# A Strassen-type output product: three pairs held for the closing part, in another order of the products

## The chip, the cores and the metric

The kernel runs on one core of a Trainium2 chip. It has a matrix engine (PE in the profile, with its weight loads as PEld), a vector engine (DVE), an activation engine (ACT), GpSimd (POOL) and SyncE (SP), which here issues nearly all transfers. The metric is the device time of one execution in microseconds; less is better.

## The reference

One transformer-like layer on x of 512 tokens by 1024, in float32. The change lies in the last line, in the product with `ffn2_w_out` (2816 by 1024):

```python
def swiglu(u, w_in, w_out):
    a, b = jnp.split(u @ w_in, 2, axis=-1)
    return (jax.nn.silu(a) * b) @ w_out
...
    u = rms_norm(x, ffn2_norm_g) * (1 + sc3) + sh3
    x = x + 0.5 * g3 * swiglu(u, ffn2_w_in, ffn2_w_out)
    return x
```

## The kernel before, in words

Every float32 product is made of three matrix products: each operand is split into a part `hi` (ACT copies it to the short float format) and a rest `lo` (DVE subtracts `hi` from the source), and `mm3` (L106) accumulates hi·hi, hi·lo and lo·hi, as lines L108, L109 and L110.

The second feed-forward block uses fewer products than the plain scheme. The hidden dimension of 2816 has 22 blocks of 128 rows, taken as 11 pairs, `i` = 0 to 10 (`NP` = 11). The tokens are taken as two halves of 256 and the output columns as two halves of 512. `pair_out` (L443) runs in two phases. In the first, three products are accumulated over the 11 pairs; their combinations P1, U2 and U4 stay on the chip. In the second phase four more products Z, Y, X and W are accumulated over the pairs, each into two PSUM banks (`tb` = 0, 1: 128 tokens by 512 columns), Z and Y in the pool `t`, X and W in the pool `g`. This second phase is what the change touches.

For each pair `prepare(i)` (L487) makes two weight tiles of 128 by 2 by 512. Tile `c` is a block of rows of the weight; its two halves feed Z and Y. Tile `d` comes from a scratch in DRAM (`ws`) with sums of weights made earlier; its halves feed W and X. Each of the two takes a load of 512 KB into a `raw` buffer, an ACT copy for `hi` and a DVE subtraction for `lo`, both in `split` (L82; ACT at L89, DVE at L91). There are 3 `raw` buffers, and 4 buffers each for `wh` and `wl`. A `raw` buffer comes free when the DVE subtraction that reads it is done. The other operand of pair `i` is `A2[i]`, which lies in a place of its own, named `A0` to `A10` (hp pool, tag `A{i}`, with a single buffer each); that place is not read any more once the second phase has gone through pair `i`.

One `step(n, tb, i, o)` is one `mm3`: three matmuls. A pair has 4 products by 2 banks, thus 24 matmuls. Pairs 0 to 8 are run one after the other. The last two pairs (`tail = 2`, L504) are the closing part: both are prepared, and then each bank gets its steps of both pairs and is finished. For a finished bank `add(src, half, tbs)` (L497) scales it with the gate (one DVE `SCALAR_TENSOR_TENSOR` at L499 from PSUM) and adds it to the residual x (one DVE `TENSOR_TENSOR` at L501 for each place), and `store` (L502) sends the finished part of x to the output (SP, L503). Z goes to one half of the columns, Y to the other, X is needed in both halves, W in one; the parts of x that X and W add to are the same for the first half.

The order in which the instructions of an engine stand is made by the scheduler of the tile framework, which moves instructions by its own estimate of when they are ready; each engine then runs its list in that order.

Of the kernel before, what the change touches and what calls it, by code (L numbers as in the profile page):

```python
# [12 lines left out]
F32R = mybir.dt.float32r  # L13
# [7 lines left out]
P = 128  # L21
# [25 lines left out]
class Layer:  # L47
# [31 lines left out]
            self.last_raw = self.nc.sync.dma_start(dst(t), src)  # L79
        return t  # L80

    def split(self, src, shape):  # L82
        nc = self.nc
        hi = self.wp.tile(shape, F32R, name=self.nm("wh"), tag="wh", bufs=4)
        lo = self.wp.tile(shape, F32R, name=self.nm("wl"), tag="wl", bufs=4)

        after = lambda i: self.tc.issue_after(i.ins) if self.lo_after else nullcontext()
        with after(self.last_uf):
            nc.scalar.activation(hi, src, AF.Copy)  # L89
        with after(self.last_ul):  # L90
            nc.vector.tensor_tensor(lo, src, hi, op=SUB)  # L91
        return hi, lo
# [350 lines left out]
    def pair_out(self, w, v, hp, tp, x_src):  # L443

        nc = self.nc
        V = nc.vector.tensor_tensor
        NP = NJ // 2
        slots = iter([f"{a}{k}" for k in range(NK) for a in ("uh", "ul")])
        new = lambda n: self.up.tile([P, 512], F32, name=self.nm(n), tag=next(slots))
        def two(*src):  # L450

            n = 2 // len(src)
            t = self.raw([P, 2, 512], [(lambda t, i=i: t[:, i:i + n, :] if n > 1 else t[:, i, :], a) for i, a in enumerate(src)])
            return self.split(t, [P, 2, 512])
        both = lambda r: w[r * P:(r + 1) * P, :].rearrange("p (h n) -> p h n", h=2)
        def one(src):
            t = self.tmp(tp, "raw1")
            nc.sync.dma_start(t, src)
            return self.split(t, [P, 512])
        def mm(ps, tb, a, b, start, stop):  # L460
            s = slice(tb * P, (tb + 1) * P)
            self.mm3(ps[tb], a[0][:, s], a[1][:, s], b[0], b[1], start, stop)

        Z, Y = [[self.tbank() for _ in range(2)] for _ in range(2)]
        X = [self.gbank() for _ in range(2)]
        for i in range(NP):
            wh, wl = two(w[2 * i * P:(2 * i + 1) * P, 0:512], self.ws[i][:, 0, :])
            w2 = one(self.ws[i][:, 2, :])
            A1 = self.A1[i]
            for ps, n, b in ((Z, 0, (wh[:, 0, :], wl[:, 0, :])), (X, 2, w2), (Y, 1, (wh[:, 1, :], wl[:, 1, :]))):  # L470
                for tb in range(2):
                    mm(ps, tb, (A1[:, n, :], A1[:, 3 + n, :]), b, i == 0, i == NP - 1)
            if i:
                self.pair_split(i - 1, hp, tp)
        P1, U2, U4 = [[new(n) for _ in range(2)] for n in ("P1", "U2", "U4")]
        for tb in range(2):
            nc.scalar.activation(P1[tb], Z[tb], AF.Copy)
        for tb in range(2):
            V(U2[tb], X[tb], P1[tb], op=ADD)
        for tb in range(2):  # L480
            V(U4[tb], Y[tb], U2[tb], op=ADD)
        self.pair_split(NP - 1, hp, tp)

        W, X = [[self.gbank() for _ in range(2)] for _ in range(2)]
        Z, Y = [[self.tbank() for _ in range(2)] for _ in range(2)]
        banks = {"Z": Z, "Y": Y, "X": X, "W": W}
        def prepare(i):  # L487
            c, d = two(both(2 * i + 1)), two(self.ws[i][:, 1:4:2, :])
            A2 = self.A2[i]
            a = lambda n: (A2[0][:, n, :], A2[1 + n // 2][:, n % 2, :])  # L490
            b = lambda n: ((c, d)[n // 2][0][:, n % 2, :], (c, d)[n // 2][1][:, n % 2, :])
            return {"Z": (a(0), b(0)), "Y": (a(3), b(1)), "X": (a(2), b(3)), "W": (a(1), b(2))}
        step = lambda n, tb, i, o: mm(banks[n], tb, *o[n], i == 0, i == NP - 1)
        g = [new("gb") for _ in range(2)]
        for h in range(2):
            nc.sync.dma_start(g[h], self.mod_d[v:v + 1, h * 512:(h + 1) * 512].to_broadcast([P, 512]))
        def add(src, half, tbs):  # L497
            t = self.tmp(tp, "rs")
            nc.vector.scalar_tensor_tensor(t, src, 0.5, g[half], op0=MUL, op1=MUL)  # L499
            for tb in tbs:  # L500
                V(self.x[tb][half], self.x[tb][half], t, op=ADD)  # L501
        def store(tb, half):  # L502
            nc.sync.dma_start(self.out[0, tb * P:(tb + 1) * P, half * 512:(half + 1) * 512], self.x[tb][half])  # L503
        tail = 2  # L504
        for i in range(NP - tail):
            o = prepare(i)
            for n in ("WZXY" if i == 0 else "ZYXW"):
                for tb in range(2):
                    step(n, tb, i, o)
            if i == 4:  # L510
                self.x_tiles()
                x_src()
            if i in (6, 7):
                tb = i - 6
                add(P1[tb], 0, (tb,))
                add(U2[tb], 0, (tb + 2,))
                add(U4[tb], 1, (tb, tb + 2))
        os = [prepare(i) for i in range(NP - tail, NP)]
        for n in "ZYXW":
            for tb in range(2):  # L520
                for i, o in enumerate(os):
                    step(n, tb, NP - tail + i, o)
                ps = banks[n][tb]
                if n == "Z":
                    add(ps, 0, (tb,))
                    store(tb, 0)
                elif n == "Y":
                    add(ps, 1, (tb,))
                    store(tb, 1)
                elif n == "X":  # L530
                    add(ps, 1, (tb + 2,))
                    store(tb + 2, 1)
                    add(ps, 0, (tb + 2,))
                else:
                    add(ps, 0, (tb + 2,))
                    store(tb + 2, 0)

    def token_gemm(self, lhs, nk, w, half, done, tail=2, extra=None, last=None):

# [801 lines left out]
```

## Time and profile before

| | |
|---|---|
| Time, median of 3 runs | 1352.87 us (1352.03 to 1353.68) |
| Profiled execution, its own time | 1351.66 us |
| Its span in the trace | 1349.8 us |
| PE busy | 1326.3 us, 98% of the span |
| DVE busy | 888.9 us, 66% |
| ACT busy | 586.0 us, 43% |
| Granted PE clock, mean | 0.998 |

The busy time of an engine counts the instructions that the profile shows on it; a matmul is shown longer than the distance between two, so the distance of the starts is what counts for PE. In the rows of the timeline the first number is the start, the second the duration, and a bracket at the end says how long the engine had been idle before and what ended that.

### The profile page before, as it was taken

How to read it: one execution, taken by the hardware profiler on the slowest of the kernel's cores; microseconds unless marked ns; L12 is line 12 of the kernel's file. 1: busy time of each engine (PE TensorE's matmuls, PEld its weight loads, DVE VectorE, ACT ScalarE, POOL GpSimd, SP SyncE). 2: the span in 40 equal slices, each digit the busy share in tenths (PEclk: the TensorE clock that was granted, in tenths of full speed). 3: DMA queues.
4: the chain of work that ended last, by engine and by line, in shares of the span. 5: the costliest groups of instructions: out<-in, count | busy, mean ns of one | idle time of the engine just before them, and what ended most of it. 6: DMA issues, size and time to landing. Idle time of an engine off the chain costs nothing.

```text
span 1349.8 us, 17806 instructions
## 1 busy us (share of the span) xinstructions
PE 1326.3 (98%) x6500; PEld 1110.5 (82%) x6500; DVE 888.9 (66%) x1668; ACT 586.0 (43%) x977; POOL 43.2 (3%) x67
## 2 busy tenths in 40 slices
PE   7999999999999999999999999999999999999997
PEld 6788887887879888888888888888788888888886
DVE  6866666655558757978786876446475555545776
ACT  4532333322235655556565676333253232223732
POOL 2000000000011011000000000002010000000000
PEclk9999999999999999999999999999999999999999
DMA  9675656665635343444243442364436777764574
GB/s 289 189 225 183 185 179 211 218 203 180 203 90 121 111 125 110 135 132 124 64 140 90 133 128 73 114 195 141 145 108 185 221 231 222 222 196 137 168 240 166
DMA packets 247291, 220.36 MB, mean 163 GB/s; under 512 B 13282, under 2 KB 208514, under 8 KB 247204
## 3 DMA queue, kind: packets, MB, share of 16 engines
q1 hardware_dynamic: 246820, 219.15, 54.1%
q8 instruction: 51, 0.84, 0.3%
q14 instruction: 36, 0.29, 0.1%
q0 software_dynamic: 320, 0.06, 0.0%
q10 hardware_dynamic: 64, 0.02, 0.0%
HBM read 195.00 MB, written 24.19 MB: 162 GB/s over the span
## 4 chain that ended last, share of the span: by engine, by line
PE 86%; DVE 7%; ACT 3%; DMA 3%; issue 1%; SPq 0%; DVEq 0%; ACTq 0%
PE g L110 23%; PE g L108 23%; PE g L109 23%; PE t L108 3%; PE t L109 3%; PE t L110 3%; PE g L693 2%; DVE wl L91 2%; PE t L1066 1%; PE t L1036 1%; DMA x<-x_d 1%; PE t L1007 1%; ACT wh L89 1%; DMA raw<-in_ffn_w_out_dram 1%; PE t L1008 1%
## 5 line engine op out<-in xcount | busy, mean ns | idle before, releaser
L89 ACT ACTIVATE wh<-raw 128x1024 fp32r<-128x1024 f32 (+2 forms) x237 | 244.4, 1036 | 434.9 <-PE g L109 144.3
L91 DVE TENSOR_TENSOR wl<-raw,wh 128x1024 fp32r<-128x1024 f32 (+2 forms) x237 | 290.3, 1227 | 190.0 <-ACT wh L89 171.0
L110 PE MATMUL g<-uh,wl 128*128 128x512 f32 (+1 forms) x976 | 366.5, 376 | 1.3 <-DVE wl L91 1.2
L108 PE MATMUL g<-uh,wh 128*128 128x512 f32 (+1 forms) x976 | 367.3, 377 | 0.2 <-ACT wh L89 0.2
L109 PE MATMUL g<-ul,wh 128*128 128x512 f32 (+1 forms) x976 | 366.5, 376 | 0.1
L110 PEld LDWEIGHTS g<-uh,wl 128*128 128x128 f32 x976 | 183.4, 188 | 35.5 <-DVE wl L91 2.2
L109 PEld LDWEIGHTS g<-ul,wh 128*128 128x128 f32 x976 | 183.6, 188 | 33.2 <-POOL ul L243 0.4
L108 PEld LDWEIGHTS g<-uh,wh 128*128 128x128 f32 x976 | 183.5, 188 | 33.2 <-ACT wh L89 0.8
L108 PE MATMUL g<-wh,uh 128*128 128x512 f32 (+2 forms) x320 | 112.3, 351 | 0.0
L110 PE MATMUL g<-wh,ul 128*128 128x512 f32 (+2 forms) x320 | 111.5, 349 | 0.0
L109 PE MATMUL g<-wl,uh 128*128 128x512 f32 (+2 forms) x320 | 111.4, 348 | 0.0
L280 DVE SCALAR_TENSOR_TENSOR acc<-raw,ccol,acc 128x1024 f32<-128x1024 f32 x49 | 62.8, 1282 | 15.4 <-DMA raw<-in_w_ada_dram 14.9
L108 PEld LDWEIGHTS g<-wh,uh 128*128 128x128 f32 x320 | 60.5, 189 | 7.8 <-DVE tk L913 0.5
L110 PEld LDWEIGHTS g<-wh,ul 128*128 128x128 f32 x320 | 60.4, 189 | 7.7
L109 PEld LDWEIGHTS g<-wl,uh 128*128 128x128 f32 x320 | 60.5, 189 | 7.3
L108 PE MATMUL g<-yh,wh 128*128 128x512 f32 x128 | 50.4, 394 | 0.0
L110 PE MATMUL g<-yh,wl 128*128 128x512 f32 x128 | 50.2, 392 | 0.0
L109 PE MATMUL g<-yl,wh 128*128 128x512 f32 x128 | 49.7, 388 | 0.0
L1018 ACT ACTIVATE S<-S,mn 128x128 f32<-128x128 f32 (+1 forms) x64 | 35.6, 557 | 16.8 <-DVE mn L1010 8.4
L109 PE MATMUL t<-wl,A 128*128 128x512 f32 x88 | 34.3, 390 | 0.8 <-DVE wl L91 0.8
L108 PE MATMUL g<-wh,hh 128*128 128x512 f32 x88 | 35.0, 398 | 0.0
L110 PE MATMUL g<-wh,hl 128*128 128x512 f32 x88 | 34.9, 397 | 0.0
(319 smaller groups left out, 2054.1 us busy)
## 6 DMA issues: line engine op xcount, KB each, us to landing
raw<-in_ffn_w_in_dram SPq DMA_DIRECT2D x82, 512.0 KB
raw<-in_w_ada_dram SPq DMA_DIRECT2D x56, 512.0 KB
raw<-in_w_mix_dram SPq DMA_DIRECT2D x46, 512.0 KB
raw<-in_ffn_w_out_dram SPq DMA_DIRECT2D x33, 512.0 KB
s<-in_ffn_w_out_dram SPq DMA_DIRECT2D x44, 256.0 KB
ws<-s SPq DMA_DIRECT2D x22, 512.0 KB
raw<-in_w_mix_dram SPq DMA_DIRECT2D x33, 256.0 KB
ar<-in_w_ada_dram SPq DMA_DIRECT2D x32, 256.0 KB
```

Source lines behind the costliest of these rows:

```text
L89: nc.scalar.activation(hi, src, AF.Copy)
L91: nc.vector.tensor_tensor(lo, src, hi, op=SUB)
L108: mm(ps, lh, rh, start=start, stop=False)
L109: mm(ps, lh, rl, start=False, stop=False)
L110: self.last_mm = mm(ps, ll, rh, start=False, stop=stop)
L280: nc.vector.scalar_tensor_tensor(acc, r, self.ccol[:, k:k + 1], acc, op0=MUL, op1=ADD)
L693: mm = nc.tensor.matmul(acc_ps[b], (wl if p == 1 else wh)[:, b % 2, s], self.ul[k] if p == 2 else self.uh[k], start=k == 0 and p == 0, sto ...
L1007: nc.tensor.matmul(ps[:, :w], q[:, s], k[:, :w], start=True, stop=False)
L1008: nc.tensor.matmul(ps[:, :w], q[:, s], kl[:, :w], start=False, stop=True)
L1018: nc.scalar.activation(S[:, ws], S[:, ws], AF.Exp, scale=-1.0, bias=m, accum_out=sm[:, qb:qb + 1])
L1036: tr = lambda b, c, qb, kb: nc.tensor.transpose(b[:, c:c + P], S[:, P_OFF[qb] + kb * P:P_OFF[qb] + (kb + 1) * P], self.ident)
L1066: nc.tensor.matmul(po[:, q0:], vt[:, kb, i, :], Px[:, o:o + T - q0], start=n == 1, stop=n == 8)
```

## The change

`tail` becomes 3, so that pairs 8, 9 and 10 are the closing part. The products of the closing part come in the order X, Z, Y, W where they came in the order Z, Y, X, W; both uses of X are added before the part of x that is then complete is stored. The split weights of pairs 8 and 9 (four tiles, `hi` and `lo` of each) no longer take the four rotating buffers of `wh` and `wl`: they go to the places `A0` to `A7` of the used-up pairs 0 to 7, and pair 10 keeps the rotating buffers.

```diff
-    def split(self, src, shape):
-        nc = self.nc
-        hi = self.wp.tile(shape, F32R, name=self.nm("wh"), tag="wh", bufs=4)
-        lo = self.wp.tile(shape, F32R, name=self.nm("wl"), tag="wl", bufs=4)
+    def split(self, src, shape, hi=None, lo=None):
+        nc = self.nc
+        if hi is None:
+            hi = self.wp.tile(shape, F32R, name=self.nm("wh"), tag="wh", bufs=4)
+            lo = self.wp.tile(shape, F32R, name=self.nm("wl"), tag="wl", bufs=4)
...
-        def two(*src):
+        def two(*src, tags=None):
 
             n = 2 // len(src)
-            t = self.raw([P, 2, 512], [(lambda t, i=i: t[:, i:i + n, :] if n > 1 else t[:, i, :], a) for i, a in enumerate(src)])
-            return self.split(t, [P, 2, 512])
+            sh = [P, 2, 512]
+            t = self.raw(sh, [(lambda t, i=i: t[:, i:i + n, :] if n > 1 else t[:, i, :], a) for i, a in enumerate(src)])
+            return self.split(t, sh, *[hp.tile(sh, F32R, name=self.nm("wt"), tag=f"A{next(tags)}", bufs=1) for _ in range(2)] if tags else ())
...
-        def prepare(i):
-            c, d = two(both(2 * i + 1)), two(self.ws[i][:, 1:4:2, :])
+        def prepare(i, tags=None):
+            c, d = two(both(2 * i + 1), tags=tags), two(self.ws[i][:, 1:4:2, :], tags=tags)
...
-        tail = 2
+        tail = 3
...
-        os = [prepare(i) for i in range(NP - tail, NP)]
-        for n in "ZYXW":
+
+        tags = iter(range(8))
+        os = [prepare(i, tags if i < NP - 1 else None) for i in range(NP - tail, NP)]
+        for n in "XZYW":
             for tb in range(2):
+                ps = banks[n][tb]
                 for i, o in enumerate(os):
                     step(n, tb, NP - tail + i, o)
-                ps = banks[n][tb]
-                if n == "Z":
-                    add(ps, 0, (tb,))
-                    store(tb, 0)
-                elif n == "Y":
-                    add(ps, 1, (tb,))
-                    store(tb, 1)
-                elif n == "X":
+                if n == "X":
                     add(ps, 1, (tb + 2,))
+                    add(ps, 0, (tb + 2,))
                     store(tb + 2, 1)
-                    add(ps, 0, (tb + 2,))
                 else:
-                    add(ps, 0, (tb + 2,))
-                    store(tb + 2, 0)
+                    half, q = {"Z": (0, tb), "Y": (1, tb), "W": (0, tb + 2)}[n]
+                    add(ps, half, (q,))
+                    store(q, half)
```

The order of instructions is the same on all engines up to the closing part. On PE the closing part begins after the 24 matmuls of pair 7. Its first rows in the changed kernel follow; `g_11443` and `g_11444` are the two banks of X, `wt_11785`/`wt_11786` are `hi`/`lo` of tile d of pair 8, `wt_11797`/`wt_11798` those of pair 9, and `wh_11809`/`wl_11810` those of pair 10:

```order
L109 MATMUL g_11443<-wt_11785,A_2033_11377 128x512
L110 MATMUL g_11443<-wt_11786,A_2033_11377 128x512
L111 MATMUL g_11443<-wt_11785,Rb_11379 128x512
L109 MATMUL g_11443<-wt_11797,A_2042_11415 128x512
L109 MATMUL g_11444<-wt_11785,A_2033_11377 128x512
L110 MATMUL g_11444<-wt_11786,A_2033_11377 128x512
L111 MATMUL g_11444<-wt_11785,Rb_11379 128x512
L110 MATMUL g_11443<-wt_11798,A_2042_11415 128x512
L111 MATMUL g_11443<-wt_11797,Rb_11417 128x512
L109 MATMUL g_11443<-wh_11809,A_2051_11434 128x512
L109 MATMUL g_11444<-wt_11797,A_2042_11415 128x512
```

Where before 24 matmuls of pair 8 stood here, led by those of Z with tile c of pair 8, X now stands first and asks for the tiles d of the three pairs; the eighth matmul reads `lo` of tile d of pair 9, and three rows further down, as fourteenth, stands the first that reads `lo` of tile d of pair 10. The place before, on PE as well, with `t_11445` and `t_11446` as the banks of Z and `wh_11779` and `wl_11780` as tile c of pair 8:

```order
L108 MATMUL t_11445<-wh_11779,A_2033_11377 128x512
L109 MATMUL t_11445<-wl_11780,A_2033_11377 128x512
L110 MATMUL t_11445<-wh_11779,Ra_11378 128x512
L108 MATMUL t_11446<-wh_11779,A_2033_11377 128x512
L109 MATMUL t_11446<-wl_11780,A_2033_11377 128x512
L110 MATMUL t_11446<-wh_11779,Ra_11378 128x512
```

These six and the 18 matmuls of Y, X and W of pair 8 stood ahead of the first use of a tile of pair 9.

On DVE the last subtractions of weights, before, in the order c and d of pair 8, c and d of pair 9, c and d of pair 10, and the first work on a finished bank (Z):

```order
L91 TENSOR_TENSOR wl_11780<-raw_11777,wh_11779 128x1024
L91 TENSOR_TENSOR wl_11786<-raw_11783,wh_11785 128x1024
L91 TENSOR_TENSOR wl_11816<-raw_11813,wh_11815 128x1024
L91 TENSOR_TENSOR wl_11822<-raw_11819,wh_11821 128x1024
L91 TENSOR_TENSOR wl_11828<-raw_11825,wh_11827 128x1024
L91 TENSOR_TENSOR wl_11834<-raw_11831,wh_11833 128x1024
L499 SCALAR_TENSOR_TENSOR rs_11843<-t_11445,gb_11449 128x512
```

The same place on DVE in the changed kernel:

```order
L92 TENSOR_TENSOR wt_11780<-raw_11777,wt_11779 128x1024
L92 TENSOR_TENSOR wt_11786<-raw_11783,wt_11785 128x1024
L92 TENSOR_TENSOR wt_11792<-raw_11789,wt_11791 128x1024
L92 TENSOR_TENSOR wl_11804<-raw_11801,wh_11803 128x1024
L92 TENSOR_TENSOR wt_11798<-raw_11795,wt_11797 128x1024
L92 TENSOR_TENSOR wl_11810<-raw_11807,wh_11809 128x1024
L501 SCALAR_TENSOR_TENSOR rs_11822<-g_11443,gb_11450 128x512
```

The subtraction of tile c of pair 10 (`wl_11804`) now stands ahead of that of tile d of pair 9 (`wt_11798`). ACT and SP keep the order of their weight copies and loads; SP's stores follow the new order of the products.

## The prediction

> **What bounds the kernel now.** I read the page first: PE is busy nearly the whole span, so only waits of PE and what runs after its last matmul can be lost or won.
>
> ```profile
> PE 1326.3 (98%) x6500; PEld 1110.5 (82%) x6500; DVE 888.9 (66%) x1668; ACT 586.0 (43%) x977; POOL 43.2 (3%) x67
> ```
>
> Then the stretches of the closing part: pair 8, the start of pairs 9 and 10, the rest of them, and the end.
>
> ```profile
> core 0: us, PE busy (x) PEld busy (x) DVE busy (x) ACT busy (x) POOL busy (x), PEclk, DMA share, GB/s
> 1325.12:1330.56 5.44, 5.44 (x25) 4.50 (x24) 3.03 (x3) 2.35 (x3) 0.00 (x0) 1.00 0.71 212
> 1342.80:1345.00 2.20, 0.00 (x0) 0.00 (x0) 2.20 (x5) 0.00 (x0) 0.00 (x0) 1.00 0.23 86
> 1345.10:1349.80 4.70, 0.00 (x0) 0.00 (x0) 1.61 (x3) 0.00 (x0) 0.00 (x0) 0.50 0.33 124
> ```
>
> Pair 8 has 24 matmuls in 5.44 us: 0.2267 us from start to start. After 1342.80 PE does nothing, and DVE is busy without a pause: the work on finished banks has piled up there. PE's and DVE's timelines give both ends of this:
>
> ```profile
> 1325.12 0.39 PE L108 MATMUL t<-wh,A 128*128 128x512 f32 x1
> ...
> 1330.56 0.39 PE L108 MATMUL t<-wh,A 128*128 128x512 f32 x1
> ...
> 1331.24 0.49 PE L108 MATMUL t<-wh,A 128*128 128x512 f32 x1
> 1332.49 0.50 PE L109 MATMUL t<-wl,A 128*128 128x512 f32 x1 [0.75 <-DVE wl L91]
> ...
> 1342.37 0.39 PE L110 MATMUL g<-wh,Ra 128*128 128x512 f32 x1
> ```
>
> ```profile
> 1324.47 1.23 DVE L91 TENSOR_TENSOR wl<-raw,wh 128x1024 fp32r<-128x1024 f32 x1 [1.78 <-ACT wh L89]
> 1325.99 1.23 DVE L91 TENSOR_TENSOR wl<-raw,wh 128x1024 fp32r<-128x1024 f32 x1 [0.30 <-ACT wh L89]
> 1328.61 1.23 DVE L91 TENSOR_TENSOR wl<-raw,wh 128x1024 fp32r<-128x1024 f32 x1 [1.39 <-ACT wh L89]
> 1331.21 1.22 DVE L91 TENSOR_TENSOR wl<-raw,wh 128x1024 fp32r<-128x1024 f32 x1 [1.38 <-ACT wh L89]
> 1333.49 1.23 DVE L91 TENSOR_TENSOR wl<-raw,wh 128x1024 fp32r<-128x1024 f32 x1 [1.05 <-ACT wh L89]
> ...
> 1344.22 1.29 DVE L499 SCALAR_TENSOR_TENSOR rs<-g,gb 128x512 f32<-128x512 f32 x2
> 1345.42 1.29 DVE L501 TENSOR_TENSOR x<-x,rs 128x512 f32<-128x512 f32 x2
> ```
>
> The last matmul ends at 1342.37 + 0.39 = 1342.76 and DVE's last addition at 1345.42 + 1.29 = 1346.71, 3.95 us later; the last store and the end of the program take the 3.1 us to the span's end at 1349.8. The five subtractions shown are, counted back from the last, `lo` of tile d of pair 8, c and d of pair 9, c and d of pair 10. PE has one wait here: the fifth matmul of the closing part starts at 1332.49 instead of at 1331.24 + 0.23, when `lo` of tile c of pair 10 (1331.21 + 1.22 = 1332.43) is there: 1.02 us.
>
> Why these tiles come so late is in ACT's timeline and in the chain of waits, here from 1325.99 on.
>
> ```profile
> 1323.38 1.06 ACT L89 ACTIVATE wh<-raw 128x1024 fp32r<-128x1024 f32 x1 [1.94 <-DMA raw<-ws]
> ...
> 1327.52 1.06 ACT L89 ACTIVATE wh<-raw 128x1024 fp32r<-128x1024 f32 x1 [1.55 <-DMA raw<-ws]
> 1330.12 1.06 ACT L89 ACTIVATE wh<-raw 128x1024 fp32r<-128x1024 f32 x1 [1.54 <-DMA raw<-in_ffn_w_out_dram]
> 1332.40 1.06 ACT L89 ACTIVATE wh<-raw 128x1024 fp32r<-128x1024 f32 x1 [1.22 <-DMA raw<-ws]
> ```
>
> ```profile
> 1325.99 1.24 DVE wl L91
> 1327.25 5.04 DMA raw<-ws
> 1332.40 1.07 ACT wh L89
> 1333.49 1.23 DVE wl L91
> 1334.72 1.20 DVE rs L499 x2
> ```
>
> ACT waits for loads, not for PE to free a split buffer. The last load starts at 1327.25, at once after the subtraction that frees its `raw` buffer, and lands 5.04 us later. The three `raw` buffers and the loads set this pace, and the change leaves buffers, order and sizes of the loads as they are. So I take all ACT and DVE times above into the changed kernel, except where DVE's order is changed.
>
> **The change part by part.** The number of matmuls, copies, subtractions, additions and transfers stays the same; places and order change.
>
> *The places.* The `wt` tiles overwrite A0 to A7, the last of which PE gives free when pair 7 is through, at 1325.12. Its writer, `lo` of tile d of pair 9, could start at 1328.61 by its data. The places cost nothing, and since ACT waited for loads here, the rotating buffers that they relieve bring nothing either.
>
> *The wait at the start of the closing part.* It begins at 1325.12, after pair 7. X asks for the tiles d. Matmul 1 has its `hi` (1323.38 + 1.06 = 1324.44); matmul 2 waits for `lo` of pair 8, until 1324.47 + 1.23 = 1325.70. Matmul 4 waits for `hi` of pair 9, until 1327.52 + 1.06 = 1328.58; matmuls 5 to 7 follow. Matmul 8 waits for `lo` of pair 9, and that stands on DVE behind `lo` of tile c of pair 10, which ends at 1332.43. At 1.22 us more it is there at 1333.65, and matmul 8 starts 0.05 us later, at 1333.70 (the distance that 1332.49 has to 1332.43). Matmul 14 needs `lo` of tile d of pair 10; on DVE it follows without a pause and ends at about 1334.88; PE is there at 1333.70 + 6 × 0.2267 = 1335.06, so this costs nothing more. All other tiles are ready. PE is idle for 1333.70 − 1325.12 − 7 × 0.2267 = 7.0 us, against 1.02 us before.
>
> *The last matmul.* From the fifth matmul of the closing part before (1332.49) to the 48th (1342.37) are 43 distances in 9.88 us, 0.2298 each with the slow restart. From matmul 8 to matmul 72 now are 64 distances: 14.71 us. The last matmul starts at 1348.41 and ends at 1348.80, 6.04 us later than before.
>
> *The pile on DVE.* A bank now takes 9 matmuls, 2.04 us, and its work on DVE two operations; two take 1.29 us by the rows above. X, with four operations for each bank, is first; its work is done while Z, Y and W keep PE busy for 54 × 0.2267 = 12.2 us. So the last bank of W is met by an idle DVE. What it costs then is shown where DVE waited for PE earlier, and where a scaling and an addition stand alone:
>
> ```profile
> 1203.86 0.39 PE L110 MATMUL g<-uh,wl 128*128 128x512 f32 x1
> ...
> 1204.35 0.69 DVE L369 TENSOR_TENSOR E<-g,sl 128x512 f32<-128x512 f32 x1 [3.11 <-PE g L110]
> ```
>
> ```profile
> 982.67 0.69 DVE L571 SCALAR_TENSOR_TENSOR rs<-g,gb 128x512 f32<-128x512 f32 x1 [2.78 <-PE g L110]
> ...
> 983.40 0.69 DVE L573 TENSOR_TENSOR x<-x,rs 128x512 f32<-128x512 f32 x1
> ```
>
> DVE starts 0.10 us after the matmul's end (1203.86 + 0.39), the addition 0.73 us after the scaling, and it takes 0.69: 1.52 us in place of 3.95, a gain of 2.43 us. The last store stays behind it; I leave it at 3.1 us. It now stands alone where two came together, for which I allow up to 0.4 us less, an estimate.
>
> *Sum without the clock.* 6.04 − 2.43 = 3.6 us more.
>
> *The clock after the wait.* The stretches show that the clock fell to 0.50 between 1345.00 and 1345.10, some 2.3 us after the last matmul. In the changed kernel PE has from 1326.2 to 1333.70 only four matmuls, 0.9 us of work in 7.5 us, with one idle piece of 4.1 us. I take the clock to fall in it. How long it stays low after the restart is shown only at the start of the program, by the same kind of instruction early and later:
>
> ```profile
> 5.67 5.16 PE L666 MATMUL t<-ident 128*128 128x128 f32 x24
> ...
> 21.45 1.91 PE L701 MATMUL t<-ident 128*128 128x128 f32 x16
> ```
>
> 24 transposes in 5.16 us are 0.215 each, 16 later ones 0.119: nearly all 24 ran slowly, so at most about 4.9 us, and a slow stretch loses 1 − 0.119/0.215 = 0.45 of its time. The price lies between 0 (no fall) and 4.9 × 0.45 = 2.2 us; I take 1.9 us, near the row of a real restart. The Trainium skill, "TensorE: Matmul & The Clock Gate", section "What's actually happening", speaks against this change: it says that an idle window of about 3.4 us halves the clock, and that a busy window of the same free-running 3.4 us restores it. By that rule the slow stretch would be one to two windows and, as an estimate, cost 1.5 to 3.0 us, a sum of 5.1 to 6.6 us. The trace agrees on the half clock, with 0.50; its fall came sooner, 2.3 us after the last matmul.
>
> *Sum.* 3.6 + 1.9 = 5.5 us more. The profiled execution took 1351.66 us and so becomes 1357.2; the median of the runs is 1.21 us above it. I give the time against the median: 1352.87 + 5.5 = 1358.4 us. About 0.2%, 2.7 us, is what a measurement of this kernel can tell from no change.
>
> **The rivals.**
>
> *The clock does not fall.* For it: four matmuls stand inside the gap. Against it: the fall at the end of the program came after less idle time. Then the time is 1352.87 + 3.6 = 1356.5 us.
>
> *Faster: the tiles come in time.* Then the last bank's gain of 2.43 us stays and the wait of 1.02 us goes: 1352.87 − 3.45 = 1349.4 us. For it: the new places take the split buffers out of the way for four tiles, and the loads differ (the first stretch moves 212 GB/s at a share of 0.71 of the DMA engines). The point from which it decides: matmul 8 would run at 1325.12 + 7 × 0.2267 = 1326.7 without a wait; below no change it comes only if `lo` of tile d of pair 9 is there 3.5 us (2.43 + 1.02) later at most, by about 1330.1, where I have 1333.65. Against it: ACT's rows name loads, and the load starts are tied to the subtractions.
>
> *Much of the wait goes, not all.* If the last loads landed 2 to 3 us sooner, the wait would shrink by as much and the clock might hold: 1352.87 + 3.6 − 2.5 = 1354.0 us, within what can't be told apart. DVE's order alone does not do that: with `lo` of pair 9 in its old place at 1328.61, matmul 14 would still wait for 1333.49 + 1.23 = 1334.72, and 58 distances later the last one starts at 1348.1, 0.3 us sooner.
>
> **How the numbers follow.** The forecast, wait and fall of the clock, 0.72; wait without the fall 0.17; the partial wait 0.06; faster 0.05. Low end: the case without the fall, less 0.84 us (the spread of the runs below their median, 1352.87 − 1352.03) and 0.4 us for the store: 1355.3. High end: 1356.5 + 2.2 for the full price of the clock + 0.81 (the spread above, 1353.68 − 1352.87) + one more subtraction of 1.22 in the way: 1360.7. The forecast lies inside, and so does most of the case without the fall; both are slower by over 0.2%, but for a part of the latter (0.02), which joins the partial wait: slower 0.87, within 0.2% 0.08, faster 0.05.
>
> **What would show it right or wrong.** In the changed profile, matmul 8 of the closing part waits for DVE's split and starts some 8 to 9 us after the end of pair 7; the two idle pieces before it are about 2.4 and 4.1 us; the granted clock shows 0.50 in the stretch after it, and matmul distances there are nearly doubled; DVE waits for PE ahead of the last scaling, and its last addition ends 1.5 us after the last matmul. It is wrong if the subtraction of tile d of pair 9 ends before 1330, if ACT's last copies start earlier than 1330.12 and 1332.40 by more than a microsecond, or if a wait for a place A0 to A7 appears.

## The result, and the profile after

The changed kernel takes 1358.04 us (median of 7 runs, 1357.21 to 1358.59), the kernel before on the same chip 1352.87 us (7 runs, 1352.03 to 1353.98): 5.17 us more, a ratio of 1.0037 with an interval of 1.0026 to 1.0049. The profiled execution took 1358.32 us, its span is 1356.5 us.

The page's row of engines hardly tells it, since PE's work is the same; 2.6 us more are booked as busy, since matmuls behind a wait or at half the clock are booked longer:

```profile
PE 1328.9 (98%) x6500; PEld 1111.5 (82%) x6500; DVE 889.1 (66%) x1668; ACT 586.3 (43%) x977; POOL 43.6 (3%) x67
```

PE's timeline of the changed kernel from the first matmul of the closing part (1326.70) to the last:

```profile
1326.70 0.39 PE L109 MATMUL g<-wt,A 128*128 128x512 f32 x1
1327.76 0.50 PE L110 MATMUL g<-wt,A 128*128 128x512 f32 x1 [0.67 <-DVE wt L92]
1328.10 0.39 PE L111 MATMUL g<-wt,Rb 128*128 128x512 f32 x1
1330.33 0.73 PE L109 MATMUL g<-wt,A 128*128 128x512 f32 x2 [1.84 <-ACT wt L90]
...
1331.14 0.39 PE L111 MATMUL g<-wt,Rb 128*128 128x512 f32 x1
1335.59 0.79 PE L110 MATMUL g<-wt,A 128*128 128x512 f32 x1 [4.07 <-DVE wt L92]
1336.18 0.63 PE L111 MATMUL g<-wt,Rb 128*128 128x512 f32 x1
1336.61 0.63 PE L109 MATMUL g<-wh,A 128*128 128x512 f32 x1
...
1351.70 0.39 PE L111 MATMUL g<-wh,Ra 128*128 128x512 f32 x1
```

The fourth matmul waits for ACT, for `hi` of tile d of pair 9; the eighth waits for DVE, for `lo` of the same tile, and starts 8.89 us after the first. After it two matmuls stand 0.43 us apart (1336.18 to 1336.61) where 0.2267 is usual. DVE's and ACT's timelines give what they waited for, and the end:

```profile
1333.18 1.23 DVE L92 TENSOR_TENSOR wl<-raw,wh 128x1024 fp32r<-128x1024 f32 x1 [4.21 <-ACT wh L90]
1334.32 1.22 DVE L92 TENSOR_TENSOR wt<-raw,wt 128x1024 fp32r<-128x1024 f32 x1
...
1352.13 0.69 DVE L501 SCALAR_TENSOR_TENSOR rs<-g,gb 128x512 f32<-128x512 f32 x1 [0.62 <-PE g L111]
1352.85 0.69 DVE L503 TENSOR_TENSOR x<-x,rs 128x512 f32<-128x512 f32 x1
```

```profile
1329.22 1.06 ACT L90 ACTIVATE wt<-raw 128x1024 fp32r<-128x1024 f32 x1 [1.52 <-DMA raw<-ws]
1332.09 1.06 ACT L90 ACTIVATE wh<-raw 128x1024 fp32r<-128x1024 f32 x1 [1.81 <-DMA raw<-in_ffn_w_out_dram]
1334.11 1.06 ACT L90 ACTIVATE wh<-raw 128x1024 fp32r<-128x1024 f32 x1 [0.96 <-DMA raw<-ws]
```

`hi` of tile d of pair 9 is there at 1329.22 + 1.06 = 1330.28. DVE then stands for 4.21 us at tile c of pair 10, whose load lands late, and takes tile d of pair 9 behind it, at 1334.32. ACT waits for loads before all three copies. At the end DVE meets the last bank idle: its last addition ends at 1352.85 + 0.69 = 1353.54, 1.45 us after the last matmul (1351.70 + 0.39 = 1352.09).

The stretches of the closing part show the clock:

```profile
core 0: us, PE busy (x) PEld busy (x) DVE busy (x) ACT busy (x) POOL busy (x), PEclk, DMA share, GB/s
1326.70:1331.53 4.83, 2.31 (x8) 0.97 (x6) 2.23 (x2) 2.06 (x2) 0.00 (x0) 1.00 0.69 195
1331.53:1335.59 4.06, 0.00 (x0) 0.00 (x0) 2.41 (x3) 2.11 (x2) 0.00 (x0) 0.55 0.37 123
1335.59:1338.74 3.15, 3.15 (x7) 2.48 (x8) 1.08 (x1) 0.00 (x0) 0.00 (x0) 0.50 0.00 0
1338.74:1351.70 12.96, 12.96 (x58) 10.72 (x57) 11.35 (x18) 0.00 (x0) 0.00 (x0) 1.00 0.32 121
```

A mean of 0.55 over the 4.06 us without a matmul means that the clock was at 0.50 for nine tenths of that time, from about 1331.9 on. It stays there for the first 3.15 us of matmuls and is back at 1338.8.

Counted from the first matmul of the closing part, the span ends 1349.8 − 1325.12 = 24.7 us later before and 1356.5 − 1326.70 = 29.8 us later after: a difference of 5.1 us in this part, as large as that of the medians. In the two profiled executions the part also starts 1.58 us later. The change does not explain that start: up to there the instructions are the same, PE's idle time in pairs 0 to 7 is 0.00 us in the profile before, 1.18 in this one and from 0.00 to 1.03 in the profiles below, and a second profile of the change (below) starts the part at 1325.42. Single runs of the kernel before spread over 4.0 to 4.4 us within each group below; that such waits make this spread is likely, but no run shows it.

### The profile page after: what moved, and what is told of

Same layout as the page of the kernel before. It is cut to its first block, busy times and chain, and to the rows that moved or that the text cites. A ratio compares the mean times of both kernels' runs of the same rounds, so it can differ in the third digit from the quotient of the medians.

```text
span 1356.5 us, 17802 instructions
## 1 busy us (share of the span) xinstructions
PE 1328.9 (98%) x6500; PEld 1111.5 (82%) x6500; DVE 889.1 (66%) x1668; ACT 586.3 (43%) x977; POOL 43.6 (3%) x67
## 4 chain that ended last, share of the span: by engine, by line
PE 88%; DVE 6%; ACT 3%; DMA 2%; issue 1%; SPq 0%; DVEq 0%; ACTq 0%
PE g L111 23%; PE g L109 23%; PE g L110 23%; PE t L109 4%; PE t L111 4%; PE t L110 4%; PE g L692 2%; PE t L1065 1%; DVE wl L92 1%; PE t L1035 1%; PE t L1006 1%; DMA x<-x_d 1%; PE t L1007 1%; DMA raw<-ws 1%; PE t L692 1%
## 5 line engine op out<-in xcount | busy, mean ns | idle before, releaser
L90 ACT ACTIVATE wh<-raw 128x1024 fp32r<-128x1024 f32 (+2 forms) x233 | 240.1, 1036 | 431.7 <-PE g L110 144.8
L92 DVE TENSOR_TENSOR wl<-raw,wh 128x1024 fp32r<-128x1024 f32 (+2 forms) x233 | 285.2, 1226 | 192.8 <-ACT wh L90 173.1
L109 PE MATMUL t<-wh,hh 128*128 128x512 f32 x88 | 34.8, 396 | 0.0
```

The source lines that it names most:

```text
L109: mm(ps, lh, rh, start=start, stop=False)
```

## The experiments

Each is compared with the kernel before on the same chip; experiments of one group share a chip. A ratio comes with its 95% interval. The first theory is the prediction's: a third pair in the closing part makes PE reach pairs 9 and 10 before their loads have landed, the clock falls in that gap, and DVE's pile at the end goes.

**Group 1** (kernel before 1352.31 us). What do order and third pair bring, each alone? First the order X, Z, Y, W with two pairs kept and no new places:

```
-        for n in "ZYXW":
+        for n in "XZYW":        # tail = 2; the additions as in the change
```

> Two pairs in the closing part as before, only the order of the products X, Z, Y, W. First theory (the pile on DVE is cleared by the longer closing part, three pairs for the same number of additions; the late tiles d cost PE whatever stands first): PE waits about 1.7 us at the start instead of 1.0, and DVE's 20 operations of 0.6 us from the first finished bank on, 12 us, still outlast PE, so that the last addition ends 0.6 us later than before: 1353.5 us. Rival (X first is by itself what clears the pile): the end comes 2.4 us earlier and the wait 0.7 later, 1351.2 us.

Measured: 1353.52 us, ratio 1.0006 (0.9997 to 1.0015): the first theory's 1353.5 us and no change both lie in the interval, the rival's 1351.2 us does not. PE's timeline of this kernel, and DVE's end:

```profile
1335.02 0.74 PE L108 MATMUL g<-wh,A 128*128 128x512 f32 x2 [1.86 <-ACT wh L89]
...
1335.90 0.63 PE L109 MATMUL t<-wl,A 128*128 128x512 f32 x1
1336.32 0.63 PE L110 MATMUL t<-wh,Ra 128*128 128x512 f32 x1
...
1346.08 0.39 PE L110 MATMUL g<-wh,Ra 128*128 128x512 f32 x1
```

```profile
1348.65 1.28 DVE L501 TENSOR_TENSOR x<-x,rs 128x512 f32<-128x512 f32 x2
```

X first brings a wait of 1.86 us for `hi` of tile d of pair 10, and even this one is followed by matmuls 0.42 apart. The pile stays: the last addition ends at 1349.93, 3.5 us after the last matmul. So the order alone does not clear the pile.

Then three pairs and the places, with the old order of products:

```
-        for n in "XZYW":
+        for n in "ZYXW":        # the rest as in the change
```

> Three pairs and the places as in the change, but the old order of the products Z, Y, X, W. First theory (the tiles come at the pace of the loads, so any order of three pairs waits): Z of pair 10 stands seventh and eighth and waits for tile c of pair 10, which DVE now does before tile d of pair 9, so the wait is one subtraction, 1.2 us, shorter than with X first; the clock falls all the same, and the pile is gone since a bank lasts 2.04 us: 1356.8 us. Rival (X first is what makes the change slow): the wait is small, and 1350 to 1352 us come out.

Measured: 1355.27 us, ratio 1.0021 (1.0012 to 1.003). PE and DVE of this kernel:

```profile
1332.03 0.79 PE L109 MATMUL t<-wh,A 128*128 128x512 f32 x1 [3.26 <-ACT wh L90]
...
1333.88 0.63 PE L111 MATMUL t<-wh,Ra 128*128 128x512 f32 x1
1334.31 0.63 PE L109 MATMUL t<-wt,A 128*128 128x512 f32 x1
...
1350.49 0.39 PE L111 MATMUL g<-wh,Ra 128*128 128x512 f32 x1
```

```profile
1350.93 0.68 DVE L501 SCALAR_TENSOR_TENSOR rs<-g,gb 128x512 f32<-128x512 f32 x1
1351.65 0.69 DVE L503 TENSOR_TENSOR x<-x,rs 128x512 f32<-128x512 f32 x1
```

The long wait and the slow matmuls are here too, now for tile c of pair 10, and the last addition ends 1.46 us after the last matmul with X in its old place. Both effects thus come from the third pair. The size was 1.5 us below the forecast of 1356.8 us, which lies just above the interval (its upper end is 1356.4). The profiled run took 1357.15 us at a mean granted clock of 0.996; eight of the ten runs have 0.997 to 0.999. This points to a clock that was low for a shorter time in most runs than in the profile.

Third, the clock by itself: the change, with X's 18 matmuls held in their order and matmuls by a tile of zeros put into PE's gaps. They add zero to a bank of X, so they only keep PE busy.

```
+        zero = self.cp.tile([P, P], F32R, name="zero")
+            for _ in range(n):   # n = 8 after X's third matmul, 17 after its seventh
+                pin(nc.tensor.matmul(X[1], zero, os[0]["X"][1][0], start=False, stop=False))
```

> The change, with 25 matmuls with a stationary operand of zeros put into the two idle pieces of PE (8 and 17), which add nothing to the bank; the order of the 18 matmuls of X is kept as it was. First theory (the fall of the granted clock costs 1.4 us): the clock stays at 1.00, the first matmuls after the wait are 0.23 us apart instead of 0.43, 1356.6 us. Rival (the restart is slow for another reason, or the clock falls anyway): 1358.0 us, as the change.

Measured: 1355.41 us, ratio 1.0021 (1.0012 to 1.0029). The stretches from X's second own matmul to its eighth, and from there to the last one:

```profile
1326.40:1334.29 7.89, 7.47 (x31) 5.66 (x32) 3.59 (x3) 3.57 (x4) 0.00 (x0) 1.00 0.51 165
1334.29:1349.25 14.96, 14.92 (x66) 11.98 (x65) 12.58 (x19) 0.36 (x1) 0.00 (x0) 1.00 0.28 106
```

In this profile the clock stays at 1.00, and from the eighth to the last matmul it takes 14.96 us in place of 16.11 (1335.59 to 1351.70), although the wait for the tiles is as it was: the eighth own matmul starts 8.70 us after the first (1325.59). By the medians this kernel is 3.1 us above the kernel before, the change 5.0 to 5.2 above its own. So the clock costs about 2 us of the 5; the intervals leave some 1.5 us of doubt, and from the eighth matmul on the profiles give 1.2 us (16.11 against 14.96) and 2.4 us (the repeat below).

Fourth, the loads: those of pair 9 go into places A0 and A1 and need no `raw` buffer; only pair 9's splits have places then (A2 to A5).

```
+            r = hp.tile(sh, F32, name=self.nm("rp"), tag=f"A{next(tags)}", bufs=1) if tags else None
-        os = [prepare(i, tags if i < NP - 1 else None) for i in range(NP - tail, NP)]
+        os = [prepare(i, tags if i == NP - 2 else None) for i in range(NP - tail, NP)]
```

> The change with other places: the loads of pair 9 go into places A0 and A1 of used-up pairs instead of the three raw buffers, its split weights into A2 to A5, those of pairs 8 and 10 into the rotating buffers. So the last four loads are issued 5 to 8 us earlier. First theory (the three raw buffers set the pace of the loads): PE's waits in the closing part shrink from 7.3 us to about 1.5, the clock stays up, and the gain at the end remains: 1350.8 us. Rival (the bytes themselves take that long, the transfers are limited by their rate): the loads issued earlier land as late as before, 1356 to 1358 us.

Measured: 1354.02 us, ratio 1.001 (1.0001 to 1.0019): between the two. ACT's copies, and the first waits of PE:

```profile
1325.77 1.06 ACT L93 ACTIVATE wt<-rp 128x1024 fp32r<-128x1024 f32 x1 [3.89 <-DMA rp<-in_ffn_w_out_dram]
1326.74 1.04 ACT L93 ACTIVATE wh<-raw 128x1024 fp32r<-128x1024 f32 x1
```

```profile
1327.83 0.80 PE L112 MATMUL g<-wh,A 128*128 128x512 f32 x1 [2.37 <-ACT wh L93]
1329.28 0.79 PE L113 MATMUL g<-wl,A 128*128 128x512 f32 x1 [0.65 <-DVE wl L95]
```

The last load is issued at 1323.17, where the change issues it at 1328.99, and the wait for pair 9 is gone. The waits of 2.37 and 0.65 us are for the two parts of tile d of pair 8, and the clock fell in the first. That tile's load was not the cause: it was issued at 1319.02, and the last update of its semaphore in the trace, which tells that it has landed, is at 1324.47, before PE asks for it at 1325.31, when pair 7 is through. But the scheduler put the copy of tile c of pair 9 ahead of its copy on ACT, and that one waited 3.89 us for its own load; DVE's subtractions stand in the same order. The stretch from 1318 to 1330 of the two kernels, this one first, then the change:

```profile
1318.00:1330.00 12.00, 8.98 (x36) 6.75 (x36) 6.58 (x6) 6.06 (x6) 0.00 (x0) 0.90 0.74 257
```

```profile
1318.00:1330.00 12.00, 9.82 (x43) 7.48 (x41) 6.92 (x7) 5.01 (x5) 0.00 (x0) 1.00 0.65 200
```

More is moved, 257 GB/s in place of 200. By the same semaphores the four loads close behind that of tile d of pair 8 each take longer, 6.1 to 7.5 us where the last four of the change take 4.3 to 5.0, but the last one still lands sooner, 5.0 us into the closing part (1330.31) where the change's lands 7.3 us into it (1334.00). So the wait that is left in this profile came by the order on ACT and DVE; no run has these early loads with the old order.

**Group 2** (kernel before 1351.98 us). The change once more, unaltered:

> The changed kernel once more, on the chip and beside the runs of the kernel before that the three other kernels of this group get. Wait, fall of the clock and the gain at the end as in its first profile: 5.2 us more than before. It also tells whether the start of the closing part, 1.6 us later than before in the first profile, belongs to the change: if not, it stands within the spread here.

Measured: 1357.01 us, ratio 1.0035 (1.0022 to 1.0047), 5.0 us more. Its profile has another share of gap and clock. PE's first, eighth and last matmul of the closing part, and the stretch behind the eighth:

```profile
1325.42 0.39 PE L109 MATMUL g<-wt,A 128*128 128x512 f32 x1
...
1333.54 0.80 PE L110 MATMUL g<-wt,A 128*128 128x512 f32 x1 [2.62 <-DVE wt L92]
...
1350.92 0.39 PE L111 MATMUL g<-wh,Ra 128*128 128x512 f32 x1
```

```profile
1333.54:1339.20 5.66, 5.66 (x13) 4.51 (x14) 3.06 (x5) 0.34 (x1) 0.00 (x0) 0.50 0.01 1
```

The eighth matmul starts 8.12 us after the first, sooner than the 8.89 above, but 13 matmuls behind it run at 0.50 in place of 7: the 64 distances to the last take 17.38 us against 16.11. The clock had fallen earlier, at about 1329.2, and stayed low longer:

```profile
1329.20:1339.40 10.20, 7.58 (x18) 5.46 (x18) 5.62 (x7) 2.11 (x2) 0.00 (x0) 0.50 0.17 55
```

Then a cure for the old pile: the kernel before, with the additions of Z and Y on GpSimd.

```
-                    add(ps, 0, (tb,))
+                    add(ps, 0, (tb,), nc.gpsimd.tensor_tensor)    # Z; the same for Y
```

> The kernel before, with the four additions of the finished banks of Z and Y on GpSimd; nothing else. It measures the pile on DVE by itself. First theory (what runs after the last matmul is DVE's pile, 20 operations of 0.6 us): 16 remain, 9.6 us from the first finished bank on, so they end about when PE's last bank is done, and the end comes 2.3 us earlier than before: 1350.0 us. Rival (the end is held by the stores and by what the program does after them): no change, 1352.3 us.

Measured: 1351.79 us, ratio 0.9996 (0.9987 to 1.0005). The gain did not come. DVE and POOL of this kernel:

```profile
1340.18 0.69 DVE L499 SCALAR_TENSOR_TENSOR rs<-g,gb 128x512 f32<-128x512 f32 x1 [0.55 <-POOL x L501]
```

```profile
1336.35 5.04 POOL L501 TENSOR_TENSOR x<-x,rs 128x512 f32<-128x512 f32 x4 [326.13 <-DVE rs L499]
```

POOL takes 1.26 us for an addition (5.04 for four), and DVE, which writes `rs` into three rotating buffers, waited for POOL to free them.

The same, with pair 10's loads in A0 and A1:

```
+            p = {10: (0, 1)}.get(i, (None, None))
```

> As the one with the additions of Z and Y on GpSimd, and besides the two loads of pair 10 go into the used-up places A0 and A1, so that they do not wait for a raw buffer: issued some 3 to 4 us earlier. First theory (the raw buffers hold these loads): PE's one wait in the closing part, 1.0 us, goes, 3.3 us less than before in all: 1349.0 us. Rival (rate of the transfers): as without the early loads, 1350.0 us.

Measured: 1351.57 us, ratio 0.9996 (0.9988 to 1.0005): no change by the runs. In the profile PE's wait at tile c of pair 10 shrank from 1.02 to 0.42 us; the last addition still ends 3.3 us after the last matmul.

Last in this group, the change with the loads of the tiles d of pairs 9 and 10, those that X asks for, put ahead by hand, behind pair 5's own loads (their splits go to A2 to A5, all others to the rotating buffers):

```
+            if i == 5:
+                preload(9, "A0")
+                preload(10, "A1")
```

> Three pairs in the closing part in the order X, Z, Y, W, but the tiles d of pairs 9 and 10, which X needs at once, are loaded far ahead into the used-up places A0 and A1 (traced behind pair 5), and split into A2 to A5; all else goes through the rotating buffers, so that only four loads are left for the last stretch. First theory (it is the late tiles that cost PE 7 us, and with them in time the gain at the end is what remains): PE waits 0.5 us in the closing part, the clock stays up, 3 us less than before: 1349.3 us. Rival (the bytes moved ahead push back the loads of the pairs before them, and PE waits there): 1352 us or more.

Measured: 1351.83 us, ratio 1.0000 (0.9991 to 1.0009), 5 us below the change. With the tiles there in time the whole loss is gone: the clock is at 1.00 throughout and the last addition ends 1.45 us after the last matmul. The stretch of the closing part, the two waits of PE that are left, and DVE ahead of the first of them:

```profile
1326.20:1344.20 18.00, 17.15 (x73) 13.43 (x72) 15.08 (x21) 2.35 (x3) 0.00 (x0) 1.00 0.30 112
```

```profile
1309.99 0.50 PE L110 MATMUL t<-wl,A 128*128 128x512 f32 x1 [0.73 <-DVE wl L92]
...
1327.75 0.50 PE L110 MATMUL g<-wl,A 128*128 128x512 f32 x1 [0.76 <-DVE wl L92]
```

```profile
1307.58 1.22 DVE L92 TENSOR_TENSOR wt<-rp,wt 128x1024 fp32r<-128x1024 f32 x1
1308.72 1.22 DVE L92 TENSOR_TENSOR wl<-raw,wh 128x1024 fp32r<-128x1024 f32 x1
```

But the first theory expected it below the kernel before, and there it isn't. In the profile the closing part itself has the gain: from its first matmul (1326.49) to the span's end (1348.6) it takes 22.1 us, against 24.7 before. It starts 1.4 us later, though. PE loses 0.9 us in pair 5, at `lo` of that pair's tile c, since the subtraction of a tile put ahead stands before it on DVE. Another 1.0 us is lost at `lo` of tile d of pair 8, where the two profiles of the change lose 0.8 and 0.3 us too, so this is not shown to come from the loads put ahead. Why the median shows no gain is open: the runs fall into two groups, five at 1350.2 to 1350.5 us, the profiled one among them, and five at 1352.8 to 1354.2, with the median alone between them.

**Group 3** (kernel before 1352.84 us). The GpSimd additions again, now with `rs` of Z and Y in places of their own:

```
+            t = self.tmp(tp, "rs") if place is None else hp.tile([P, 512], F32, name=self.nm("rs"), tag=f"A{place}", bufs=1)
```

> The kernel before with the four additions of Z and Y on GpSimd again, but the scaled banks for them lie in the used-up places A2 to A5 and not in the three rotating buffers, for which DVE waited 0.55 us at a time in the earlier run of this kind. First theory (DVE's pile of 20 operations of 0.6 us sets the end, and that run failed by these buffers alone): 16 operations, 9.6 us from the first finished bank on, end 2.3 us earlier than before: the last addition about 1.7 us after the last matmul in place of 3.95, 1349.8 us. Rival (GpSimd slows DVE, or something else holds the end): the last addition over 3.5 us after the last matmul, 1352 us.

Measured: 1351.59 us, ratio 0.9993 (0.9984 to 1.0002). DVE no longer waits for POOL, but for PE:

```profile
1338.95 1.29 DVE L499 SCALAR_TENSOR_TENSOR rs<-g,gb 128x512 f32<-128x512 f32 x2 [0.67 <-PE g L110]
...
1345.18 1.28 DVE L501 TENSOR_TENSOR x<-x,rs 128x512 f32<-128x512 f32 x2
```

My theory of the pile was mis-sized. Not Z's and Y's operations fill the end, but the twelve of X and W: X's first bank is finished at about 1338.9, where DVE had waited 0.67 us for it, twelve operations at about 0.6 us are 7.2 us, and here they take 7.5, to 1346.46, whatever was done before.

So one addition of X goes to GpSimd too, and pair 10's loads into A0 and A1:

```
+                    add(ps, 1, (tb + 2,), 6 + tb)    # X, on GpSimd
+            p = {10: (0, 1)}.get(i, (None, None))
```

> The same, with one of the two additions of X on GpSimd too (places A6 and A7), and the two loads of pair 10 into A0 and A1 as in the run with early loads. First theory: both losses of the kernel before, the wait of 1.0 us at the start and the pile of 2.4 us at the end, go: 3.2 us less than before, 1349.0 us. Rival (spread of the loads eats it): within 1 us of the kernel before.

Measured: 1350.77 us, ratio 0.9986 (0.9977 to 0.9994): 2.1 us below the kernel before, and the fastest version here. Its last addition ends 2.6 us after the last matmul (1344.50 against 1341.88) in place of 3.95. Expected were 3.2 us. The wait at the start is all but gone in the profile (0.1 us), the pile is shorter by 1.3 us of the 2.4 hoped for; six additions take POOL 8.01 us, and DVE is at times slower beside them (below).

The places alone, with two pairs and the old order (pair 9's splits in A0 to A3):

> The kernel before with one part of the change alone: the split weights of pair 9 go to the places A0 to A3 of used-up pairs; two pairs in the closing part, order Z, Y, X, W. First theory (the split buffers hold nothing back here, ACT waits for loads): no change, 1352.3 us. Rival (a free split buffer lets loads start earlier): the wait of 1.0 us goes, 1351.3 us.

Measured: 1352.51 us, ratio 1.0000 (0.9992 to 1.0009). These four of the change's eight places cost and bring nothing.

Last, DVE's order: the change, with pair 10's splits held behind pair 9's.

```
+        with self.tc.issue_after(self.last_lo.ins):
+            os.append(prepare(NP - 1))
```

> The changed kernel with the weight splits of pair 10 behind those of pair 9 on DVE, so that tile d of pair 9 no longer stands behind tile c of pair 10. First theory (the last load is the floor): PE reaches the products of pair 9 some 4 us earlier, but then waits for tile d of pair 10, and the last matmul comes 0.3 us earlier than in the change: 5 us more than before, 1357.0 us. Rival (DVE's order made the wait): 3 us less than the change, 1354.3 us.

Measured: 1357.11 us, ratio 1.0033 (1.002 to 1.0045). PE of this kernel:

```profile
1329.42 0.80 PE L110 MATMUL g<-wt,A 128*128 128x512 f32 x1 [0.27 <-DVE wt L92]
...
1333.46 0.79 PE L109 MATMUL g<-wh,A 128*128 128x512 f32 x1 [2.82 <-ACT wh L90]
```

The wait for `lo` of tile d of pair 9 is only 0.27 us now, and the next one, for `hi` of tile d of pair 10, is 2.82. DVE's order only chooses at which tile PE stands; the loads set how long.

## Why the prediction was right, step by step

The forecast of 1358.4 us is 0.4 above the median. That it came so near is in part luck: in each of the two profiles the wait and the clock are off by 0.3 to 0.8 us, in opposite directions. By its terms, each counted from the first matmul of the closing part:

| term | forecast | first profile | repeat |
|---|---|---|---|
| matmul 1 to 8, less 7 × 0.2267 | 7.0 us | 8.89 − 1.59 = 7.30 | 8.12 − 1.59 = 6.53 |
| matmul 8 to 72 | 14.71 + 1.9 | 16.11 = 14.71 + 1.40 | 17.38 = 14.71 + 2.67 |
| last matmul's end to last addition's | 1.52 | 1.45 | 1.45 |
| closing part, start to span's end, above before | 5.5 | 5.1 | 5.7 |

- *The wait.* Right, with its place, the tile and the cause. The idle pieces before the eighth matmul were forecast at about 2.4 and 4.1 us; they are 2.0 (1328.33 to 1330.33) and 4.2 (1331.37 to 1335.59). The copies of the last tiles start 2.52, 5.39 and 7.41 us into the part, and 2.40, 5.00 and 7.28 before: taking ACT's times over unchanged was right to 0.4 us. The run with the tiles d put ahead shows that it is these tiles: with them there in time, 5 us go.
- *The pile on DVE.* Right: a gain of 3.95 − 1.45 = 2.50 us, forecast 2.43. The old-order run shows that it is the third pair that gives it, not X in front. The text gave both reasons together; only one was needed.
- *The places.* Right as far as tested: the places-only run, with pair 9's splits alone, shows no difference, and no wait for a place appears in the rows of the change.
- *The store at the end.* From the last addition to the span's end it takes 2.96 us against 3.09; the 0.4 us allowed for it was hardly needed.
- *The clock.* The mechanism was right, and the filled gaps show it. The size was less certain than the bounds said: 1.40 and 2.67 us in two profiles of the same kernel, the second above my upper bound of 2.2. The failed reason is the comparison with the program's start: it gave at most 4.9 us of slow matmuls after the restart. In the first profile the clock was low for 6.8 us, of which the gap hid the first 3.6, and 3.2 us were paid; in the repeat it was low for 10.2 us, and 5.9 us came after the restart (1333.54 to 1339.4). So the price has no single size. By medians, with the filled run, it is about 2 us, near the 1.9 taken. The Trainium skill, "TensorE: Matmul & The Clock Gate", section "What's actually happening", has the windows of 3413 ns run free of the program; two of them are the 6.8 us, three the 10.2, and the estimate of 1.5 to 3.0 us that I had worked out from it holds 2.67, and misses 1.40 by little.
- *The rivals.* That the tiles come in time, or that the clock holds, is refuted by the waits and the 0.50 in both profiles. What I priced at 0.3 us, DVE's order, measured +4.3 us over before where the change has +5.0 to 5.2: the same within the spread.

What stays open: what the early loads of pair 9 bring when ACT and DVE keep their order, and why the run with the tiles d put ahead shows no gain in its median.

## What to carry to other kernels

Keeping more work for a closing part helps the engine that cleans up at the end, but it also moves the first use of the last tiles forward; compare the time at which each will be asked for with the time at which its load lands now, before counting the gain. A wait of a few microseconds on TensorE can cost more than its length, here 1.4 and 2.7 us more in two profiles of one kernel. Loads put ahead take longer side by side, and the copies and subtractions that belong to them can come to stand ahead of those needed first; look at the order on each engine again. An addition handed to another engine only helps if it is one of those that stand in the last stretch.

## What the runs showed of the hardware

- The clock fell 2.3 us after the last matmul at the end of the kernel before, and 0.4 us after four matmuls between two idle pieces in the first profile (1331.5 against 1331.9); in the repeat it fell while these four ran, and in the order-only run 0.7 us after PE had restarted from a gap of 2.0 us. So neither the length of a gap alone nor its end says when it falls.
- Low stretches within a kernel lasted 3.41 us (order only), 6.83 us (first profile, early loads) or 10.24 us (repeat, old order, DVE's order): one, two or three times 3.41 us.
- An estimate of how much work keeps the clock up: cut each profile's last part into windows of 3.413 us from its own changes of clock, and count a matmul as 0.2267 us, at half clock as 0.426. In the first profile the four matmuls fill 0.27 of the window before the fall. In all 14 profiles the clock fell after windows that were filled to at most 0.38 and held after those filled to 0.44 or more; it came back after windows filled to 0.88 or more, and not at 0.70 or less. Where these windows lie against the gap, which differed between the two profiles of the changed kernel, would then decide what is paid.
- In the filled run 25 matmuls by zero held the clock at 1.00.
- GpSimd took 1.26 us for an addition of 128x512 where DVE takes 0.69, and DVE's own operations stretched at times beside it, in the fastest version:

```profile
1339.80 0.97 DVE L506 TENSOR_TENSOR x<-x,rs 128x512 f32<-128x512 f32 x1
```

```profile
1333.92 8.01 POOL L506 TENSOR_TENSOR x<-x,rs 128x512 f32<-128x512 f32 x6 [323.53 <-DVE rs L504]
```

The addition at 1339.80, while POOL is still at its six, takes 0.97 us; one alone takes 0.69, as the last of the changed kernel at 1352.85.
